# Splits of weights put off by slices, an inverse root in ten steps, casts one per block, coefficients, stabilizer and memory heads placed anew

## The chip, the cores and the metric

The kernel runs on one core of a Trainium2 chip. The metric is the device time of one execution in microseconds; the time of the kernel before is the median of three runs. A NeuronCore has five engines that each take their instructions strictly in the order in which they were written and wait for one another through semaphores: PE (matrix products), DVE and POOL (vectors), ACT (functions and copies) and SP (which here only issues DMA). The order in each engine's queue is therefore part of the kernel, and this change is above all a change of order.

## The reference, cut to what matters

512 tokens of width 1024, in fp32, pass through two transformer blocks.

```python
def first_block(x, ...):
    h = rms_norm(x, attn_norm)
    sb_q, sb_k, sb_v, cq, ckv, k_pe = split(h @ w_in)
    sb  = stick_breaking_attention(sb_q, sb_k, sb_v)          # 8 heads of 64
    mla = chunk_causal_softmax_attention(q, k, v)             # from cq @ w_uq, ckv @ w_ukv, norms, rope
    x = x + concat(rms_norm(sb), rms_norm(mla)) @ w_o
    return x + peer_ffn(rms_norm(x, ffn_norm), ...)           # 16384 experts, 8 heads x top 16

def peer_ffn(h, w_q, sub_keys, u, v):
    sc = einsum(h @ w_q, sub_keys)                            # scores of 2 x 128 keys a head
    idx, g = top 16 of the sums of the two top-16 lists, softmax of their scores
    coef = g * gelu(h . u[idx])
    return sum over k of coef[k] * v[idx[k]]

def second_block(x, c, ...):
    sh1, sc1, g1, sh2, sc2, g2 = split(silu(c) @ w_ada + b_ada)
    hn = rms(x) * (1 + sc1) + sh1
    y  = concat(fox(hn), mlstm(hn), moba(hn))                 # 6 + 4 + 6 heads of 64
    x  = x + g1 * (y @ w_out)
    hn = rms(x) * (1 + sc2) + sh2
    gate, up = split(hn @ w_gate_up)
    return x + g2 * ((silu(gate) * up) @ w_down)
```

`rms_norm` divides by the root of the mean square. The four `mlstm` heads ("memory heads") weigh a product of queries and keys by exp(logd - m), where m, the stabilizer, is a running maximum along the tokens.

## The kernel before

**Products.** An fp32 operand is written as hi + lo, two rounded parts, and `mm3` (L338) makes one product of three matmuls: hi by hi, hi by lo, lo by hi. Weights come through one object, `Stream`: `_load` (L192) has SP issue a DMA of a 128x1024 tile into one of four buffers, `high` (L201) casts it to `whi` on ACT, `_split` (L211) subtracts to make `wlo` on DVE or, for some tiles, on POOL. `get` for tile i splits up to tile i+2 (LOOK = 2), loads up to tile i+5, and then calls `ada_tick`, which advances `ada_gen`: this forms the six modulation vectors of the second block on POOL from tiles `ada_w` that SP loads as well (L638), a unit for each weight tile. `tok_gen` (tokens on partitions) and `feat_gen` (features on partitions) are the generators that take a weight tile and yield after each product of 128 rows of it, a slice; other work is put between slices.

**Norms.** `rsqrt_gen` (L344) makes 1/sqrt on DVE in twelve dependent steps: scale and add, an integer shift, a first guess by a subtraction, three Newton rounds of three steps each. The class `Norm` uses it twice for each of the four row norms: once for three token tiles together (`early`), once for the last tile (`late`).

**The expert layer.** 384 tokens go through all 16384 experts as dense products, with a coefficient that is zero where an expert wasn't chosen; the other 128 tokens gather their rows by indirect DMA. Before the long loop over the 128 first keys stands a stage of 48 blocks (16 for each of three token tiles, `g_hot` and `g_sum`) that builds the matrix of gates G by one-hot products and writes it to memory (`gs` to `gdram`, L1181). Beside the blocks run three steps a block of `decode(1)`, then `decode(2)`, which turn top-k positions into indices on DVE; `spread(2)` (L1044), four ACT casts of indices of 128x1024, is called at block 10. After the stage come `u_next(len(early))`, which makes the first products with u, then loads, then `c_tile(0)` (L1257), which makes the first tile of coefficients: `ch` on ACT, `cl` on DVE. The first product with v needs both.

**The attention of the second block.** 52 items (24 of fox attention, 24 of MoBA, 4 memory heads, put in at the places `ML_AT`) run through `run_pipe`: the parts of an item have lags, counted in items, and between them a `Fill` object takes slices of the generator `behind()`, up to a number of nanoseconds for each item. `behind()` ends with: the stabilizer (`am` on DVE L1547, transposes on PE L1551, a scan on DVE L1553, transposes on PE L1557), the projections `mqk` and `mvo`, the functions silu and sigmoid on ACT, the transposes `y_T(0..4)` (L1536) of the finished parts of y, the first half of the output product. A memory head has a part e (a copy `sel` on DVE L1619, one matmul L1621 that spreads row h of the maximum, four exponentials on ACT), four parts z (a matmul L1634 and a product on DVE L1637 each) and a part v (ten matmuls, L1644).

## Time and profile before

| | |
|---|---|
| runs | 2362.58 us median (2351.52, 2362.58, 2366.8) |
| profiled execution, own time | 2349.11 us |
| its span in the profile | 2347.1 us |
| mean granted clock of PE | 0.979 |
| busy: PE, DVE, ACT, POOL | 2254.4, 1565.1, 964.1, 1008.3 us |

A line of the timeline gives the start, the busy time of the instructions grouped in it, engine, source line, operation, tile written <- tiles read, and in brackets how long the engine stood idle just before and which instruction of which line ended that. A line of the waits adds these up. A clock of 1.00 is 2.4 GHz, 0.50 is 1.2 GHz.

### The profile page before, as it was taken

How to read it: one execution, taken by the hardware profiler on the slowest of the kernel's cores; microseconds unless marked ns; L12 is line 12 of the kernel's file. 1: busy time of each engine (PE TensorE's matmuls, PEld its weight loads, DVE VectorE, ACT ScalarE, POOL GpSimd, SP SyncE). 2: the span in 40 equal slices, each digit the busy share in tenths (PEclk: the TensorE clock that was granted, in tenths of full speed). 3: DMA queues.
4: the chain of work that ended last, by engine and by line, in shares of the span. 5: the costliest groups of instructions: out<-in, count | busy, mean ns of one | idle time of the engine just before them, and what ended most of it. 6: DMA issues, size and time to landing. Idle time of an engine off the chain costs nothing.

```text
span 2347.1 us, 31805 instructions
## 1 busy us (share of the span) xinstructions
PE 2254.4 (96%) x11721; PEld 1935.9 (82%) x11721; DVE 1565.1 (67%) x3005; ACT 964.1 (41%) x1712; POOL 1008.3 (43%) x665
## 2 busy tenths in 40 slices
PE   7999999988989999999999999998999898999999
PEld 6887778988988888888888888888987666888787
DVE  5667659999948888888887888775655245333332
ACT  4567434457843333333333333335543424222211
POOL 5750034620036667676666767624775002600000
PEclk9999999999999999999999999999999879999999
DMA  5430232335798898988989988853442002433231
GB/s 178 140 111 1 81 101 96 102 135 200 283 322 308 308 323 308 317 319 305 347 306 311 321 317 297 308 178 97 138 141 83 29 24 81 153 99 98 86 112 54
DMA packets 175800, 441.09 MB, mean 188 GB/s; under 512 B 17052, under 2 KB 71964, under 8 KB 172572
## 3 DMA queue, kind: packets, MB, share of 16 engines
q1 hardware_dynamic: 136620, 301.87, 38.2%
q0 software_dynamic: 36864, 134.23, 15.7%
q10 hardware_dynamic: 2160, 2.95, 0.5%
q8 instruction: 92, 1.51, 0.3%
q14 instruction: 64, 0.52, 0.1%
HBM read 406.69 MB, written 32.31 MB: 187 GB/s over the span
## 4 chain that ended last, share of the span: by engine, by line
PE 63%; DVE 4%; ACT 3%; issue 2%; DMA 2%; POOL 1%; SPq 0%; ACTq 0%; POOLq 0%; DVEq 0%
PE bank L340 19%; PE bank L342 19%; PE bank L341 19%; PE bank L593 1%; PE bank L582 1%; DVE wlo L211 1%; POOL rows L1286 1%; DVE ohAB L1151 1%; DMA w<-in_peer_v_dram 1%; ACT whi L201 1%; PE bank L574 1%; POOL wlo L211 1%; PE bank L1644 0%; DVE ohA L1158 0%; ACT ohA L1161 0%
## 5 line engine op out<-in xcount | busy, mean ns | idle before, releaser
L340 PE MATMUL bank<-hhi,whi 128*128 128x384 f32 (+1 forms) x1600 | 580.2, 363 | 0.1
L342 PE MATMUL bank<-hhi,wlo 128*128 128x384 f32 (+1 forms) x1600 | 574.3, 359 | 5.7 <-POOL wlo L211 5.7
L341 PE MATMUL bank<-hlo,whi 128*128 128x384 f32 (+1 forms) x1600 | 571.5, 357 | 1.5 <-DVE hlo L466 1.4
L211 POOL TENSOR_TENSOR wlo<-w,whi 128x1024 fp32r<-128x1024 f32 (+2 forms) x128 | 322.0, 2520 | 568.5 <-ACT whi L201 519.4
L201 ACT CAST whi<-w 128x1024 fp32r<-128x1024 f32 (+4 forms) x414 | 421.7, 1024 | 304.1 <-PE bank L342 157.1
L211 DVE TENSOR_TENSOR wlo<-w,whi 128x1024 fp32r<-128x1024 f32 (+3 forms) x286 | 348.4, 1220 | 256.8 <-ACT whi L201 255.9
L342 PEld LDWEIGHTS bank<-hhi,wlo 128*128 128x128 f32 x1600 | 302.8, 189 | 33.7 <-POOL wlo L211 8.7
L340 PEld LDWEIGHTS bank<-hhi,whi 128*128 128x128 f32 x1600 | 302.9, 189 | 31.6 <-issue 4.2
L341 PEld LDWEIGHTS bank<-hlo,whi 128*128 128x128 f32 x1600 | 302.8, 189 | 29.7 <-DVE hlo L466 2.5
L340 PE MATMUL bank<-whi,ch 128*128 128x512 f32 x768 | 303.9, 396 | 5.8 <-ACT ch L1257 4.3
L341 PE MATMUL bank<-wlo,ch 128*128 128x512 f32 x768 | 304.0, 396 | 1.6 <-DVE wlo L211 1.6
L342 PE MATMUL bank<-whi,cl 128*128 128x512 f32 x768 | 304.2, 396 | 0.0
L1264 DVE TENSOR_TENSOR cl<-ge,ch 128x384 fp32r<-128x384 f32 x125 | 145.5, 1164 | 140.2 <-ACT ch L1263 140.2
L1286 POOL DMA_INDIRECT rows<-in_peer_v_dram,eidx x128 | 186.6, 1458 | 119.8 <-DVE acc L1309 87.9
L1286 POOL DMA_INDIRECT rows<-in_peer_u_dram,eidx x128 | 177.4, 1386 | 85.9 <-DVE junk L1304 62.6
L1304 DVE SCALAR_TENSOR_TENSOR junk<-rows,h 128x1024 bf16<-128x1024 f32 x128 | 186.4, 1456 | 0.3
L655 POOL TENSOR_SCALAR ada_w<-ada_w,c_c 128x512 f32<-128x512 f32 x84 | 155.9, 1856 | 70.6 <-DMA ada_w<-in_w_ada_dram 70.5
L1309 DVE SCALAR_TENSOR_TENSOR acc<-rows,coefg,acc 128x1024 f32<-128x1024 f32 x127 | 181.5, 1429 | 0.3
L340 PEld LDWEIGHTS bank<-whi,ch 128*128 128x128 f32 x768 | 144.6, 188 | 37.5 <-ACT ch L1257 4.7
L340 PE MATMUL bank<-whi,hhi 128*128 128x384 f32 (+3 forms) x448 | 174.0, 388 | 0.3 <-ACT whi L201 0.3
L342 PEld LDWEIGHTS bank<-whi,cl 128*128 128x128 f32 x768 | 144.5, 188 | 35.7 <-DVE cl L1264 0.8
L951 ACT ACTIVATE ge<-bank 128x384 f32<-128x384 f32 x113 | 55.7, 493 | 286.1 <-PE bank L342 284.7
(385 smaller groups left out, 3465.9 us busy)
## 6 DMA issues: line engine op xcount, KB each, us to landing
w<-in_uT_dram SPq DMA_DIRECT2D x128, 512.0 KB
w<-in_peer_v_dram SPq DMA_DIRECT2D x128, 512.0 KB
ada_w<-in_w_ada_dram SPq DMA_DIRECT2D x96, 256.0 KB
gdram<-gs SPq DMA_DIRECT2D x24, 1024.0 KB
gblk<-gdram SPq DMA_DIRECT2D x16, 1536.0 KB
w<-in_w_gu_dram SPq DMA_DIRECT2D x44, 512.0 KB
w<-in_w_down_dram SPq DMA_DIRECT2D x22, 512.0 KB
w<-in_w_pq_dram SPq DMA_DIRECT2D x16, 512.0 KB
```

Source lines behind the costliest of these rows:

```text
L201: nc.scalar.copy(hi[:, :n], self.loaded[i][:, :n])
L211: (eng or nc.vector).tensor_tensor(lo[:, :n], t[:, :n], hi[:, :n].bitcast(F32), op=OP.subtract)
L340: nc.tensor.matmul(o, ah, bh, start=start, stop=False)
L341: nc.tensor.matmul(o, ah, bl, start=False, stop=False)
L342: nc.tensor.matmul(o, al, bh, start=False, stop=stop)
L574: nc.tensor.transpose(bt[:, si * P:(si + 1) * P], src()[:, si * P:(si + 1) * P], ident)
L655: nc.gpsimd.tensor_scalar(w, w, col_, None, op0=OP.mult)
L951: nc.scalar.activation(t, b[:, :DTOK], AF.Gelu)
L1264: nc.vector.tensor_sub(cl, t, ch.bitcast(F32))
L1286: nc.gpsimd.indirect_dma_start(out=r, out_offset=None, in_=A["peer_" + kind], in_offset=bass.IndirectOffsetOnAxis(ap=eidx[:, k:k + 1], axi ...
L1304: nc.vector.scalar_tensor_tensor(junk, r, 1.0, h2, op0=OP.mult, op1=OP.mult, accum_out=preg[:, k:k + 1])
L1309: nc.vector.scalar_tensor_tensor(acc, r, coefg[:, k:k + 1], acc, op0=OP.mult, op1=OP.add)
```

## The change

- `Stream.get` has an argument `later`, set by `feat_gen` and by `tok_gen` (but for the last two tiles of an output that is finished token tile by token tile): the cast of tile i+2 is then written behind the first slice, its subtraction and the next load behind the third. The load of tile i+5 so stands behind the `ada_w` load of `ada_tick` in SP's queue.
- `rsqrt_gen`: the shift and the guess become one step; for up to 16 columns the three rounds become a round of five steps with a cubic correction and one of three. Twelve steps become ten, or eleven for wider inputs.
- `spread` becomes a generator: one cast for each of the four blocks from block 10 on, and `decode(2)` makes its first steps behind them.
- `c_tile(0)` stands ahead of `u_next` and of the loads.
- The stabilizer is taken out of its place in `behind()` and put between the slices of `mqk`: `am` ahead of the first slice, the first transposes four slices later, the second ten slices after that.
- Memory heads one item earlier; `sel` becomes a part of its own at lag 0; e, z and v one lag later (1, 3 and 4); `y_T(3)` and `y_T(4)` two MoBA items later.

```diff
-ML_AT = (45, 47, 49, 51)
+ML_AT = (44, 46, 48, 50)
...
+        def step(self):
+            if self.todo:
+                self.todo.pop(0)()
+        def get(self, key, ahead=LOOK, later=False):
...
+            while self.todo:
+                self.step()
             for k in range(i, i + ahead + 1):
-                self._split(k)
-                self._load(k + DEEP - 1)
+                if later and k == i + ahead:
+                    self.todo = [lambda k=k: self.high(k), lambda: None,
+                                 lambda k=k: (self._split(k), self._load(k + DEEP - 1))]
+                else:
+                    self._split(k)
+                    self._load(k + DEEP - 1)
...
-        nc.vector.tensor_scalar(u, v.bitcast(I32), 1, None, op0=OP.logical_shift_right)
-        yield
-        nc.vector.tensor_scalar(u, u, -1.0, 1597463007.0, op0=OP.mult, op1=OP.add)
+        nc.vector.tensor_scalar(u, v.bitcast(I32), -0.5, 1597463007.0, op0=OP.mult, op1=OP.add)
...
-        for k in range(3):
+        cubic = n <= 16
+        for k in range(2 if cubic else 3):
...
+            if cubic and k == 0:
+                nc.vector.tensor_scalar(w, t, 1.5, 2.5, op0=OP.mult, op1=OP.add)
+                yield
+                nc.vector.tensor_mul(t, w, t)
+                yield
...
-            for _ in range(3):
-                next(d, None)
+            if next(sp, sp) is sp:
+                for _ in range(DSTEP):
+                    next(d, None)
...
+        c_tile(0)
         u_next(len(early))
         load_g(0)
         nc.sync.dma_start(h2, x1d[DT])
         bcast_row(acc, A["ffn_norm_row"], D)
-        c_tile(0)
...
-                yield from feat_gen(("mqk", j), hhi, hlo, KC, lambda b: nc.scalar.copy(cv[:, 3:S + 3], b))
+                for ns in feat_gen(("mqk", j), hhi, hlo, KC, lambda b: nc.scalar.copy(cv[:, 3:S + 3], b)):
+                    yield ns
+                    next(st, None)
...
-                yield lambda c=c: step["moba"] >= 8 * (c - 2)
+                yield lambda c=c: step["moba"] >= 8 * (c - 2) + 2
...
-            return [(0, e_part)] + [(2, lambda si=si: z_part(si)) for si in range(NT)] + [(3, v_part)]
+            return ([(0, sel_part), (1, e_part)] + [(3, lambda si=si: z_part(si)) for si in range(NT)] +
+                    [(4, v_part)])
```

Three places show how the order moves. The first is PE's queue at the entry of the memory heads; `ident,y` are the transposes of `y_T`, four each, `mT,sel` is part e, `whi,hhi` and its two neighbours are slices of the other projections, `bv,at_pT`, `ident,at_s` and `kTb,qTb` are MoBA items. Before:

```order
L1536 MATMUL bank<-ident,y 128x128 x8
L582 MATMUL bank<-bv,at_pT 128x64 x4
L574 MATMUL bank<-ident,at_s 128x128 x2
L593 MATMUL bank<-kTb,qTb 128x128
L1536 MATMUL bank<-ident,y 128x128 x12
L644 MATMUL bank<-ones,ada_a 128x1 x4
L340 MATMUL bank<-whi,hhi 128x512
L341 MATMUL bank<-wlo,hhi 128x512
L342 MATMUL bank<-whi,hlo 128x512
L582 MATMUL bank<-bv,at_pT 128x64
L574 MATMUL bank<-ident,at_s 128x128 x3
L1621 MATMUL bank<-mT,sel 128x512
```

Of the change:

```order
L1564 MATMUL bank<-ident,y 128x128 x12
L603 MATMUL bank<-bv,at_pT 128x64 x4
L595 MATMUL bank<-ident,at_s 128x128 x2
L1564 MATMUL bank<-ident,y 128x128 x4
L665 MATMUL bank<-ones,ada_a 128x1 x4
L603 MATMUL bank<-bv,at_pT 128x64
L595 MATMUL bank<-ident,at_s 128x128 x3
L1659 MATMUL bank<-mT,sel 128x512
L614 MATMUL bank<-kTb,qTb 128x128
L603 MATMUL bank<-bv,at_pT 128x64 x2
L595 MATMUL bank<-ident,at_s 128x128 x4
L1564 MATMUL bank<-ident,y 128x128 x4
```

All five groups of transposes stood ahead of the first part e; now the last of them stands behind it, and the slice that stood between them has moved behind the last.

The second place is PE's queue around the stabilizer; `ident,am` and `ident,mT` are its two groups of transposes. Before, two small attention matmuls lie between them:

```order
L593 MATMUL bank<-kTf,qTf 128x512
L1551 MATMUL bank<-ident,am 4x128 x4
L582 MATMUL bank<-fv,at_pT 128x64 x4
L574 MATMUL bank<-ident,at_s 128x128 x2
L593 MATMUL bank<-kTb,qTb 128x128
L1557 MATMUL bank<-ident,mT 128x4 x4
L340 MATMUL bank<-hhi,whi 128x512
```

Of the change, the first group stands among slices of `mqk`, and the second some forty rows further on:

```order
L353 MATMUL bank<-hhi,whi 128x512
L354 MATMUL bank<-hlo,whi 128x512
L355 MATMUL bank<-hhi,wlo 128x512
L1575 MATMUL bank<-ident,am 4x128 x4
L353 MATMUL bank<-hhi,whi 128x512
L354 MATMUL bank<-hlo,whi 128x512
L355 MATMUL bank<-hhi,wlo 128x512
```

Between the two groups there are now ten slices of three matmuls each.

The third is ACT's queue behind the stage of G; `gs` are the last copies of G, `ge` is the gelu of a product with u, `whi` the cast of a weight tile and `ch` the coefficient tile; the numbers are those of buffers. Before:

```order
L1179 COPY gs<-bank 128x128x4 x4
L201 CAST whi<-w_7210 128x1024
L951 ACTIVATE ge<-bank 128x384
L201 CAST whi<-w_7304 128x1024
L951 ACTIVATE ge<-bank 128x384
L1257 ACTIVATE ch<-ge_3318 128x384 x2
L201 CAST whi<-w_7398 128x1024
```

Of the change:

```order
L1204 COPY gs<-bank 128x128x4 x4
L1285 ACTIVATE ch<-ge_3300 128x384
L203 CAST whi<-w_7202 128x1024
L972 ACTIVATE ge<-bank 128x384
L203 CAST whi<-w_7296 128x1024
L972 ACTIVATE ge<-bank 128x384
L1285 ACTIVATE ch<-ge_3300 128x384
```

Two casts and two gelus that stood ahead of the first `ch` now stand behind it.

## Rows read from the trace of the kernel before

**Rows 1.** The page, parts 1 and 5: busy; group, busy, mean ns, idle ahead.

```profile
PE 2254.4 (96%) x11721; PEld 1935.9 (82%) x11721; DVE 1565.1 (67%) x3005; ACT 964.1 (41%) x1712; POOL 1008.3 (43%) x665
...
L340 PE MATMUL bank<-hhi,whi 128*128 128x384 f32 (+1 forms) x1600 | 580.2, 363 | 0.1
```

**Rows 2.** PE's waits: tile and line, what ended the wait: us, times, longest.

```profile
PE bank L434 <- DVE rs_u L349: 22.8, 4, 12.6
PE bank L1536 <- DVE y L604: 7.8, 1, 7.8
...
PE bank L1177 <- ACT ohA L1161: 3.5, 1, 3.5
...
PE bank L340 <- ACT ch L1257: 4.3, 1, 4.3
...
PE bank L1385 <- DVE dg L1391: 2.5, 1, 2.5
...
PE bank L1621 <- DVE sel L1619: 1.9, 3, 0.7
...
PE bank L1557 <- DVE mT L1553: 1.2, 1, 1.2
...
PE bank L1551 <- DVE am L1547: 1.1, 1, 1.1
```

**Rows 3.** Windows: stretch, its length, busy us by engine, clock, DMA share, GB/s.

```profile
538.00:570.00 32.00, 27.97 (x204) 25.70 (x204) 31.12 (x47) 21.85 (x51) 0.00 (x0) 0.89 0.52 182
570.00:660.00 90.00, 89.18 (x822) 85.66 (x821) 81.67 (x106) 71.22 (x167) 0.00 (x0) 1.00 0.77 282
1745.00:1749.00 4.00, 2.08 (x16) 1.65 (x16) 3.24 (x6) 2.60 (x7) 3.80 (x5) 0.99 0.22 71
1749.00:1762.40 13.40, 13.01 (x41) 10.30 (x42) 4.01 (x14) 2.62 (x7) 2.90 (x2) 0.50 0.25 79
1846.40:1861.40 15.00, 15.00 (x44) 10.74 (x44) 4.33 (x13) 6.09 (x14) 1.15 (x4) 0.50 0.11 35
1861.40:1878.60 17.20, 15.13 (x72) 10.03 (x71) 6.79 (x22) 3.96 (x9) 1.14 (x4) 1.00 0.09 31
1878.60:1902.30 23.70, 23.13 (x61) 15.04 (x60) 4.72 (x17) 5.47 (x13) 3.74 (x10) 0.50 0.00 0
1902.30:1922.40 20.10, 17.23 (x97) 12.96 (x96) 9.71 (x35) 2.95 (x5) 1.47 (x2) 0.99 0.09 27
```

**Rows 4.** Timeline of DVE in a norm: first and last of nine chain steps.

```profile
309.25 0.16 DVE L351 TENSOR_SCALAR rs_u<-rs_u 128x3 int32<-128x3 int32 x1
...
311.01 0.16 DVE L360 SCALAR_TENSOR_TENSOR nr_r<-rs_t,nr_r 128x3 f32<-128x3 f32 x1
```

**Rows 5.** Timeline of ACT in the stage of G.

```profile
532.61 3.88 ACT L1044 CAST tir<-topi 128x1024 f16<-128x1024 uint32 x4
```

**Rows 6.** Timeline of ACT at the first coefficient tile.

```profile
672.64 0.94 ACT L1257 ACTIVATE ch<-ge 128x384 fp32r<-128x384 f32 x2 [3.25 <-DMA gdram<-gs]
```

**Rows 7.** Timeline of PE there: the second product with v.

```profile
685.30 0.50 PE L341 MATMUL bank<-wlo,ch 128*128 128x512 f32 x1 [1.60 <-DVE wlo L211]
```

**Rows 8.** Timeline of PE behind the stabilizer: one matmul after the other.

```profile
1750.47 0.63 PE L341 MATMUL bank<-hlo,whi 128*128 128x512 f32 x1
1750.90 0.63 PE L342 MATMUL bank<-hhi,wlo 128*128 128x512 f32 x1
```

**Rows 9.** Timeline of PE in a slice ahead of the memory heads.

```profile
1833.56 0.40 PE L341 MATMUL bank<-wlo,hhi 128*128 128x512 f32 x1
1833.80 0.39 PE L342 MATMUL bank<-whi,hlo 128*128 128x512 f32 x1
```

**Rows 10.** Timeline of DVE at the entry of the memory heads.

```profile
1843.70 1.29 DVE L1538 TENSOR_TENSOR hlo<-bank,hhi 128x512 fp32r<-128x512 f32 x2 [9.48 <-ACT hhi L1537]
```

**Rows 11.** Timeline of DVE ahead of the output of the mixer.

```profile
2195.16 1.23 DVE L211 TENSOR_TENSOR wlo<-w,whi 128x1024 fp32r<-128x1024 f32 x1 [0.25 <-ACT whi L201]
```

**Rows 12.** SP's waits between 1600 and 1850 us.

```profile
SPq L638 <- POOL ada_a L656: 115.8, 33, 18.7
```

More of the change, by code (lines that the diff above doesn't have):

```diff
@@ L68 @@
 PREP_N = 10
+DSTEP = 3
 LOOK = 2
@@ L480, in block @@
                     cp == cps[0] and ci == 0, cp == cps[-1] and ci == per - 1)
+                W.step()
                 yield 3 * N / 2.4
         for cp in cps[:-2] if split else cps:
-            w = W.get((key, cp))
+            w = W.get((key, cp), later=True)
             if not b:
@@ L507, in feat_gen @@
     def feat_gen(key, hi, lo, kc, evac, n=S):
-        wh, wl = W.get(key)
+        wh, wl = W.get(key, later=True)
         b = bank()
@@ L512, in feat_gen @@
             mm3(b[:, :n], (wh[:, w_], wl[:, w_]), (hi[:, c, :n], lo[:, c, :n]), c == 0, c == kc - 1)
+            W.step()
             yield 3 * n / 2.4
@@ L1211, in build @@
                 if tt == 0:
-                    spread(2)
+                    sp = spread_gen(2)
+                    next(sp)
                     ij1, d = decode(2)
@@ L1538, in y_T, with stabilizer @@
             nc.vector.tensor_sub(hlo[:, c, :], b, hhi[:, c, :].bitcast(F32))
+        def stabilizer():
+            nc.vector.tensor_sub(am, gt[:, :, 6:10], cum[:, :, 10:14])
+            for _ in range(4):
+                yield
+            b = bank()
+            for tt in range(NT):
+                nc.tensor.transpose(b[:MLH, tt * P:(tt + 1) * P], am[:, tt, :], ident)
+            nc.vector.tensor_copy(mT, b[:MLH, :])
+            nc.vector.tensor_tensor_scan(out=mT, data0=mT, data1=mT, initial=0.0, op0=OP.max, op1=OP.max)
+            for _ in range(10):
+                yield
+            b = bank()
+            for tt in range(NT):
+                nc.tensor.transpose(b[:, tt * MLH:(tt + 1) * MLH], mT[:, tt * P:(tt + 1) * P], ident[:MLH, :MLH])
+            nc.vector.tensor_add(em, b[:, :16].rearrange("p (t h) -> p t h", t=NT), cum[:, :, 10:14])
+            nc.scalar.activation(em, em, AF.Exp, scale=-1.0)
         def behind():
@@ L1566, in behind @@
             nc.gpsimd.memset(mv1[:, :, :, 64:65], 1.0)
+            st = stabilizer()
             for j in range(4):
```

38 lines of the change are left out of this document (16 added, 22 removed).

## The prediction

> **What bounds the kernel now.** I read the busy times first: PE is busy 2254.4 us of a span of 2347.1 [rows 1], so only 93 us can come back from its waits, and besides them only what it loses at half clock. Then PE's waits one by one, because what the change touches is worth something only where PE stands still: the longest single kinds that it touches are norms, the entry of the memory heads, the first coefficient, and waits of 1 to 3.5 us in between [rows 2]. Then the windows with the granted clock, because behind some of these waits PE runs for 13 to 24 us at 0.50 [rows 3]. The reader is to see that a short wait can be followed by a loss larger than itself. In the long expert loop PE doesn't wait, and the order of all engines there is unchanged, so that part cannot move.
>
> **Norms.** The chain on DVE has nine steps from 309.25 to 311.01, that is (311.01 - 309.25)/9 = 0.195 us a step [rows 4]. A norm has 3 and 1 columns, both below 16, so each of its two chains loses two steps. PE waits for both chains (four waits, 22.8 us in all, begin with one [rows 2]). Per norm 2 x 2 x 0.195 = 0.78, for four norms **-3.1**. Bounds: the late chains lie between other DVE work, so at worst only the early ones count, -1.6; at best a step that waits behind a longer one goes too, -4.
>
> **Stage of G.** Four casts on ACT take 3.88 us in one piece [rows 5], and PE waits 3.5 for the one-hot rows that ACT forms behind them [rows 2]. One cast a block is 3.88/4 = 0.97, and ACT has room: from 538 to 570 it works 21.85 of 32. But DVE works 31.12 of these 32 and PE 27.97, so in this stretch DVE sets the pace, and later, from 570 to 660, PE does (89.18 of 90) [rows 3]. The wait can be saved only so far as DVE follows; its steps of `decode(2)` begin four blocks later, into the stretch where PE leads and hides them. **-3**; bounds 0 (DVE is the bound anyway) and -5 (clock 0.89 there becomes 1).
>
> **First coefficients.** `ch` waits for the last store of `gs` [rows 6], since its tile takes memory from which that store reads; this store isn't sooner, so neither is `ch`. Now ACT, which takes its work strictly in order, holds two casts and two gelus behind it. The first product with v, at about 673 before, behind this `ch`, would come a cast and a gelu or two later, 1 to 2 us. But the second product with v waits for its own `wlo` until 685.30 [rows 7], and that one depends on none of this: the delay goes into its wait of 1.60. **+0.5**; bounds -4.3 (the whole wait of [rows 2], if the store is not what holds it) and +3.
>
> **Stabilizer.** PE waits 1.1 for `am` and 1.2 for the scan [rows 2], 2.3 together. Now four slices and ten slices lie between. Behind these waits it runs 13.4 us at clock 0.50 [rows 3]. A matmul there goes on after 1750.90 - 1750.47 = 0.43 us [rows 8], elsewhere after 1833.80 - 1833.56 = 0.24, or 0.233 over several [rows 9]: a ratio of 1.83. At full clock the 13.01 us of work are 7.1. So 2.3 + 13.4 - 7.1 = **-8.6**; if the clock falls all the same, -2.3.
>
> **Memory heads.** Before, the stretch from the end of PE's work at 1846.4 - 7.8 = 1838.6 to 1922.4 is 83.8 us. The wait of 7.8 [rows 2] stems from ACT: silu, sigmoid and their tables stand ahead of the casts `hhi` of the transposes, and DVE stood still 9.48 us for these before its two `hlo` at 1843.70 [rows 10]. That stays. In the new order PE does more transposes and one MoBA step, and stops where it needs the bank (accumulator tile) of the first transposes, free after the first `hlo`, 1843.70 + 0.65 = 1844.35: a wait of about 5.8, followed by some 1.3 for `sel`, which stands behind three `hlo` (0.65 each). Then comes the work. At full clock the four windows hold 15.00/1.83 + 15.13 + 23.13/1.83 + 17.23 = 53.2 [rows 3]. The first of the two half-clock stretches follows the long wait, which remains, so I leave its loss: 15.00 - 8.2 = 6.8. The second, 23.7 us, came behind three waits of 0.65 to 0.72 for `sel` and for the exponentials, of which rows 2 list `sel` with 1.9. In the new order `sel` is copied an item sooner and slices stand between e, z and v, so I let it go. Of the small waits in these windows, (17.20 - 15.13) + (23.70 - 23.13) + (20.10 - 17.23 - 2.3) = 3.2, I leave a third, 1.0. The 2.3 at the end is a wait for the norm of the heads' result; its chain has 16 columns and loses two steps, 0.4, and begins an item sooner, for which I take off half of the rest: 0.95 stays. Sum 5.8 + 1.3 + 53.2 + 6.8 + 1.0 + 0.95 = 69.0, so **-14.8**. If the second stretch recurs, its loss of 23.1 - 12.6 = 10.5 stays and the term is -4.3.
>
> **Output's modulation.** PE waits 2.5 for `dg` [rows 2], behind a `wlo` of 1.23 [rows 11]; the first two `dg` now stand ahead of it. **-1.4** (with the gap ahead of it); bound 0.
>
> **Splits put off.** The same casts, subtractions and loads, later by one to three slices of 0.7 us (three matmuls [rows 9]). A tile is split two tiles before its use, so PE doesn't see it: **0**. Bounds -2 (PE waits for hi or lo of a slice that no longer stand behind it) and +2 (a subtraction now stands ahead of an attention step). The loads are the third rival.
>
> **Sum.** -3.1 - 3 + 0.5 - 8.6 - 14.8 - 1.4 = -30.4 on the profiled execution of 2349.1 (span 2347.1 and 2.0 around it), so 2318.7 on its own scale. That execution is 13.5 us faster than the median of the runs; against the median I predict 2362.6 - 30.4 = **2332**.
>
> **A rule against it.** The clock part of the sum, 6.3 at the stabilizer (13.4 - 7.1) and 10.5 in the heads, rests on waits of 1.25 us and less that end in half clock; the rows show the falls right behind such waits, at 1749 and at 1878.6, with no longer wait near [rows 2, 3]. The Trainium skill ("TensorE: Matmul & The Clock Gate", section "HAM oscillation") lays a fall to long idle gaps of PE, as where a kernel waits for a transfer between its tiles. By it these two falls would not come from these waits and would not go with them, and the sum would be -30.4 + 16.8 = -13.6. The same page's section on a second failure mode knows falls from many short idles, and there the rows agree, so the page doesn't decide.
>
> **Rivals.**
> 1. *The clock falls anyway*, and not from these waits. PE's work around the falls is narrow: transposes of 4 columns, a matmul with 4 rows, products of 64 rows. If that lowers the clock and not the waits, it falls in the new order too, since these matmuls are all still there. For it: they stand at both places. Against it: from 1861.4 to 1878.6 the same kinds ran at 1.00 [rows 3]. Then both losses remain: -30.4 + 6.3 + 10.5 = -13.6: 2349.
> 2. *Only the heads' second fall recurs*, because z, now one lag later, waits for the exponentials elsewhere. The 1.9 for `sel` [rows 2] would be gone, but ACT still does its sixteen exponentials in the stretch, and their waits were of the same size. -30.4 + 10.5 = -19.9: 2343.
> 3. *Loads come late* (the other side). Some sixty loads of weights stand one `ada_w` load later on SP, and SP waits for POOL's `ada_a` 115.8 us in 33 waits, 3.5 each, at most 18.7 [rows 12]. A load is issued three tiles before its cast; a tile is 8 slices of 0.7, so the lead is some 17 us, less the transfer. A mean wait fits into it, the longest doesn't. If each of sixty loads lost the mean 3.5 with no lead left, it were +210; it decides against the change from 30 + 24 = 54 us on, which is 16 loads with a bare 3.5 each: some 2390. Against it: ahead of its 1600 products of the commonest form PE waited 0.1 us in all [rows 1], so weights are now far from late.
> 4. *The edits do little*: PE's stops move on to the next bank or the next table load, as the entry of the memory heads shows already, and only norms, `dg` and a part of G stay: -3.1 - 1.4 - 3 = -7.5: 2355.
>
> **Chances.** The forecast, all of the sum: 0.45, by itself 2320 to 2342. Rival 1: 0.20; rival 2: 0.18; rival 3: 0.06; rival 4: 0.11. For the range, 2312 takes in the best bounds (-4, -5 and -4.3 instead of -3.1, -3 and +0.5, and the medians' scatter), 2357 the fourth rival. About 1% is what a measurement of this kernel can tell from no change, here 24 us: faster below 2339, slower above 2386. Of the forecast some 0.37 lie below 2339, of rival 2 0.07, of rival 1 0.05: faster 0.49; slower is rival 3, 0.06; the rest is within 1%, 0.45.
>
> **What would show it.** Right: PE's waits for `am` and mT gone and the clock 1.00 in the slices of `mqk`; at the entry of the memory heads one wait near 6 us for a bank, then one half-clock stretch, and none in the middle of the heads; norm waits for `rs_u` shorter by 0.4 each time; no wait of 3.5 for `ohA`; `ch` still behind the last store. Wrong: half clock again behind the stabilizer or in the middle of the heads (rivals 1 and 2); PE's waits for `whi` or `wlo` with a DMA ahead of them (rival 3); the same total of PE's waits under new names (rival 4).

## The result, and the profile after

The changed kernel took 2338.02 us, median of four runs (2319.21 to 2347.63), against 2360.3 for the kernel before (2351.52 to 2366.8): ratio 0.9899, 95% interval 0.9858 to 0.9941. 2332 was forecast, with a range of 2312 to 2357. On two further occasions, six runs each, its medians were 2334.6 and 2329.9, ratios 0.9885 [0.9839, 0.9931] and 0.9871 [0.9828, 0.9915]. Of the 165 runs below, six, all of edited kernels and two of them the changed kernel's (2365.32 and 2362.87), lie more than 1.5% above the fastest of their kernel and are left out of the means as slow; with them the changed kernel's mean would be 2336.9 instead of 2333.0 us and its time at half clock 97.7 instead of 88.7.

The profiled execution has a span of 2336.9 us, 10.2 shorter than the one before, with a mean clock of 0.980. Page, part 1:

```profile
PE 2252.1 (96%) x11721; PEld 1934.5 (83%) x11721; DVE 1562.1 (67%) x2973; ACT 964.8 (41%) x1712; POOL 1000.4 (43%) x665
```

PE's waits (tile and line, what ended the wait: us in all, times, longest). These answer to [rows 2]; the line numbers of the change are 2 to 38 higher.

```profile
PE bank L453 <- DVE rs_u L362: 21.2, 4, 12.1
...
PE bank L595 <- DVE hlo L1566: 6.4, 1, 6.4
...
PE bank L353 <- ACT whi L203: 5.7, 2, 5.4
PE bank L354 <- DVE wlo L213: 5.3, 4, 3.5
...
PE bank L1564 <- DVE y L1645: 1.2, 1, 1.2
...
PE bank L1413 <- DVE dg L1419: 1.0, 1, 1.0
```

The four waits of the norms fell from 22.8 to 21.2, `dg` from 2.5 to 1.0, the heads' last norm from 2.3 to 1.2; `am`, mT, `sel` and the wait of 3.5 for ACT's `ohA` are gone from the list (PE's waits for DVE's `ohA` grew from 7.4 to 9.1 in all). New are 5.4 for `whi` and 3.5 for `wlo` at the first coefficients, where 4.3 for `ch` and 1.6 for `wlo` stood, and the entry of the heads still waits, 6.4 instead of 7.8, now in one go for `hlo`.

Windows of the same execution (stretch, length, busy us by engine, granted clock, DMA share, GB/s), to be read beside [rows 3]: a stretch of the first block that ran at 1.00 before; the slices of `mqk` with the stabilizer; the first half of PE's stand at the entry of the heads (1853.8 to 1860.2); the stretch at 0.50 that begins in this stand; the one behind it.

```profile
211.80:246.00 34.20, 34.20 (x119) 22.57 (x119) 20.29 (x50) 16.66 (x40) 0.00 (x0) 0.50 0.00 1
1744.00:1770.00 26.00, 26.00 (x170) 23.96 (x170) 14.82 (x51) 12.96 (x31) 19.73 (x14) 1.00 0.52 173
1853.80:1857.10 3.30, 0.04 (x1) 0.00 (x0) 0.00 (x0) 3.27 (x6) 0.00 (x0) 0.99 0.00 0
1857.10:1867.30 10.20, 6.52 (x20) 4.42 (x21) 4.55 (x16) 8.62 (x20) 3.95 (x8) 0.50 0.00 0
1867.30:1916.40 49.10, 47.81 (x245) 34.21 (x245) 23.46 (x76) 14.30 (x31) 7.29 (x16) 1.00 0.10 30
```

Behind the stabilizer the clock is 1.00, in the heads 10 us are at 0.50 instead of 44 (before 20.5 from 1841.1 on, in the wait that [rows 3] leaves out, and 23.9 from 1878.6 on), but 34.2 us of the first block's stick-breaking attention ran at 0.50. This stretch hides most of the gain in the profiled execution. So the first thing to find out was which of these stretches belong to the kernel and which to the execution.

### The profile page after: what moved, and what is told of

Same layout as the page of the kernel before. It is cut to its first block, busy times and chain, and to the rows that moved or that the text cites. A ratio compares the mean times of both kernels' runs of the same rounds, so it can differ in the third digit from the quotient of the medians.

```text
span 2336.9 us, 31771 instructions
## 1 busy us (share of the span) xinstructions
PE 2252.1 (96%) x11721; PEld 1934.5 (83%) x11721; DVE 1562.1 (67%) x2973; ACT 964.8 (41%) x1712; POOL 1000.4 (43%) x665
## 4 chain that ended last, share of the span: by engine, by line
PE 79%; DVE 9%; ACT 4%; issue 3%; DMA 3%; POOL 2%; SPq 0%; ACTq 0%; POOLq 0%; DVEq 0%
PE bank L353 23%; PE bank L355 22%; PE bank L354 22%; PE bank L603 2%; PE bank L614 2%; DVE wlo L213 2%; PE bank L595 1%; DMA w<-in_peer_v_dram 1%; DVE ohAB L1176 1%; PE bank L866 1%; DVE ohA L1183 1%; ACT whi L203 1%; POOL rows L1314 1%; POOL wlo L213 1%; PE bank L1051 1%
## 5 line engine op out<-in xcount | busy, mean ns | idle before, releaser
L676 POOL TENSOR_SCALAR ada_w<-ada_w,c_c 128x512 f32<-128x512 f32 x84 | 149.3, 1778 | 75.4 <-DMA ada_w<-in_w_ada_dram 74.9
L354 PEld LDWEIGHTS bank<-wlo,ch 128*128 128x128 f32 x768 | 145.0, 189 | 37.3 <-DVE wlo L213 5.0
```

The costliest lines, as they stand in the source:

```text
L354: nc.tensor.matmul(o, ah, bl, start=False, stop=False)
L676: nc.gpsimd.tensor_scalar(w, w, col_, None, op0=OP.mult)
```

## How the runs are read

Every run lists its span and its mean granted clock c. PE has two levels, so 2(1 - c) times the span is the time it spent at 0.50. Over the 159 runs of all kernels below, with a constant of its own for each kernel, a microsecond at 0.50 goes with 0.447 us of span (standard error 0.012), and the runs scatter by 2.8 us around that line. The difference of two kernels can so be split into a part at half clock and the rest, which is work and waits. In one kernel alone the half clock varies so much (the changed kernel's first four runs have clocks from 0.977 to 0.988, some 108 to 56 us at half clock) that a median over few runs moves by 10 us. "±" is one standard error.

| kernel | runs | mean us | at half clock | rest, against before |
|---|---|---|---|---|
| before | 61 | 2357.4 ± 1.1 | 125.6 ± 2.4 | 0 |
| changed (3 occasions) | 14 | 2333.0 ± 2.6 | 88.7 ± 5.2 | -7.6 ± 0.9 |
| changed, c_tile(0) back | 10 | 2332.4 ± 3.0 | 91.0 ± 6.2 | -9.2 ± 1.0 |
| changed, splits in one piece | 10 | 2335.5 ± 3.6 | 94.8 ± 6.4 | -7.8 ± 1.0 |
| before + stabilizer | 12 | 2352.1 ± 2.4 | 118.4 ± 5.8 | -1.7 ± 0.9 |
| before + heads | 11 | 2343.8 ± 2.7 | 109.1 ± 5.8 | -5.9 ± 0.9 |
| before + both | 12 | 2345.7 ± 2.2 | 116.1 ± 4.5 | -7.2 ± 0.9 |
| pick (e7, e10) | 12 | 2321.6 ± 2.4 | 73.5 ± 5.0 | -12.2 ± 1.1 |
| pick + entry (e8, e11) | 12 | 2324.1 ± 3.1 | 84.5 ± 5.9 | -14.6 ± 1.0 |
| pick + entry + two steps (e9) | 5 | 2320.5 ± 4.3 | 73.3 ± 10.6 | -13.3 ± 1.5 |

The kernel before had 129.3 ± 3.8, 119.3 ± 3.7 and 129.9 ± 5.1 us at half clock on its three occasions (e1 to e4; e5 to e8; e9 to e12), so the half clock of a kernel that ran on one occasion is compared with the runs of before from there.

The second table is worked out from the traces, one of each label: the time between the starts of two products of PE that stand in every kernel, in brackets the us of it at clock 0.50. A: from the first product of the first block to the first score of its attention. B: from there to the first product behind the next norm. G: the stage of G. C: from the end of that stage to the thirteenth slice with v. L: from there to the last slice with v. N: from the first product of the second block to the first of fox attention with values. S: around the stabilizer. H: from the end of the slices before the heads to the last slice of the mixer's output of the first half. F: the gated FFN's first two thirds.

| trace | A | B | G | C | L | N | S | H | F |
|---|---|---|---|---|---|---|---|---|---|
| before | 129.5 | 168.5 (9) | 169.9 (10) | 33.2 (3) | 893.1 | 81.0 | 69.1 (14) | 121.1 (48) | 228.9 |
| changed | 130.9 | 183.1 (43) | 167.9 (12) | 38.6 (10) | 896.5 | 82.0 | 60.8 | 98.2 (10) | 227.0 |
| e1_again | 131.9 (3) | 167.8 (10) | 168.7 (7) | 38.6 (10) | 894.1 | 82.2 | 60.8 | 113.9 (44) | 226.8 |
| e12_again2 | 130.8 | 183.1 (43) | 167.9 (12) | 38.6 (10) | 894.1 | 82.7 (2) | 60.8 | 102.0 (20) | 226.8 |
| e2_ctile_back | 132.3 (3) | 183.1 (43) | 167.9 (9) | 33.5 (7) | 897.2 | 82.4 (1) | 60.8 | 98.6 (10) | 226.8 |
| e3_split_back | 128.3 | 167.7 (9) | 167.9 (9) | 38.6 (10) | 893.3 | 79.4 | 60.8 | 103.3 (20) | 228.3 (1) |
| e4_stab_heads | 129.0 | 183.9 (43) | 169.5 (16) | 33.0 (3) | 894.9 | 80.0 (1) | 60.9 | 118.4 (51) | 228.9 |
| e5_stab_only | 129.0 | 168.3 (10) | 170.2 (14) | 33.6 (3) | 893.9 | 82.8 (3) | 60.8 | 124.8 (55) | 228.9 (1) |
| e6_heads_only | 129.3 | 183.9 (44) | 170.2 (14) | 33.2 (3) | 894.8 | 82.5 (3) | 62.6 | 111.3 (38) | 228.2 |
| e7_pick | 128.8 | 167.1 (7) | 168.4 (10) | 33.1 (7) | 896.2 | 79.9 (1) | 60.8 | 103.3 (20) | 226.8 (1) |
| e10_pick2 | 128.5 | 167.3 (7) | 168.5 (10) | 33.4 (7) | 896.2 | 79.8 (1) | 60.8 | 100.6 (14) | 226.8 (1) |
| e8_entry | 127.7 | 183.1 (43) | 167.9 (9) | 33.5 (7) | 900.0 (3) | 81.0 | 60.8 | 107.4 (34) | 228.6 |
| e11_entry2 | 129.3 | 167.8 (9) | 167.9 (9) | 33.4 (7) | 894.4 | 79.4 | 60.8 | 97.7 (14) | 227.1 |
| e9_steps2 | 128.8 | 167.8 (8) | 168.3 (9) | 33.5 (7) | 894.4 | 79.3 | 60.8 | 97.9 (14) | 227.1 |

## The experiments

### The changed kernel again (e1_again, e12_again2)

No edit.

> The changed kernel once more, nothing edited. In its first trace PE ran 34.1 us at clock 0.50 from about 210 us on, in the stick-breaking attention of the first block, behind a wait of 0.51 us for at_pT; the kernel before has the same wait of 0.51 us at 208.8 us and stayed at 1.00. Theory 'chance of the run': the stretch is there in some executions and not in others, so here it is likely absent from the profile or the runs spread by some 15 us with the mean clock (0.988 without it, about 0.978 with it). Theory 'made by the change' (splits put off shift the work around it): the stretch is there again at 210 us, and no run comes under 2330.

> The changed kernel once more, for a third trace of it. The stretch of 34 us at half clock at 210 us stood in five of ten traces so far, whatever the first block's edits; the fall of the clock in the heads between 10 and 51 us with the new steps. If both are chance, the trace may have either; 37 to 40 us around the first coefficients (30.8 to 33.5 with c_tile back) and 60.8 around the stabilizer must be there again.

Measured: medians 2334.64 (six runs) and 2329.85 (six runs), ratios 0.9885 and 0.9871. The stretch of 34 us is absent from the first of these traces and there in the second (column B: 10, then 43). The first trace of the changed kernel and this one show the same program; windows of e1_again, same columns as above, the first of them the stretch that ran at 0.50 in the first trace, the others in the memory heads:

```profile
211.80:246.00 34.20, 34.15 (x216) 23.17 (x215) 31.14 (x73) 25.50 (x66) 0.00 (x0) 1.00 0.00 1
1837.40:1851.00 13.60, 9.35 (x29) 6.67 (x29) 5.24 (x17) 10.65 (x21) 3.96 (x8) 0.50 0.00 0
1851.00:1854.50 3.50, 3.50 (x14) 2.06 (x13) 1.73 (x4) 0.00 (x0) 0.00 (x0) 0.99 0.00 0
1854.50:1878.30 23.80, 23.80 (x64) 15.94 (x64) 6.48 (x21) 5.35 (x14) 3.99 (x9) 0.50 0.07 23
```

In the first block 34.2 us run at 1.00 here and at 0.50 there, with PE busy 34.15 and 34.20 of them. So that stretch is chance of the execution: over the fourteen traces it stands in six, among them e4 and e6, whose first block is that of the kernel before word for word. It begins 2.0 to 2.5 us behind a wait of half a microsecond; but that wait stands in all fourteen traces, so it doesn't decide. The first trace of the changed kernel, and this one:

```profile
209.36 0.43 PE L603 MATMUL bank<-sbv,at_pT 128*128 128x64 f32 x2 [0.51 <-ACT at_pT L597]
209.64 0.43 PE L603 MATMUL bank<-sbv,at_pT 128*128 128x64 f32 x2 [0.50 <-ACT at_pT L597]
```

The heads are the other way round: this execution ran 23.8 us at 0.50 from 1854.5 on where the first had 1.00, with PE busy every microsecond. PE's timeline ahead of that fall:

```profile
1842.55 2.04 PE L1659 MATMUL bank<-mT,sel 4*128 4x512 f32 x2 [0.57 <-ACT at_pT L597]
...
1851.42 2.42 PE L1672 MATMUL bank<-mqk 64*128 64x512 f32 x8
1853.77 1.45 PE L1659 MATMUL bank<-mT,sel 4*128 4x512 f32 x2
1855.15 1.22 PE L614 MATMUL bank<-kTb,qTb 64*128 64x256 f32 x2
1856.30 0.79 PE L353 MATMUL bank<-whi,hhi 128*128 128x512 f32 x1
```

The last wait of a quarter of a microsecond or more, 0.57, lies 12 us ahead of the fall at 1854.4. Between them PE worked on products of the heads and of attention with no wait above 0.15 us. This fall had no wait right in front of it.

Most falls do have one. Counted over the fourteen traces, from 20 us on to 8 us before the end, each of the 76 waits of PE of 2.7 us or more has a fall of the clock in it or at most 2.1 us behind it; of the 48 waits of 2.0 to 2.7 us that weren't at half clock anyway 33 have one, of the 136 of 1 to 2 us 24. Of all 155 falls 132 stand at such waits. The half clock at long waits is so there in every execution; the stretches of 24 and 34 us, which make executions differ most, have no wait above 0.72 us in the 11 us ahead of them.

### c_tile(0) put back (e2_ctile_back)

```diff
-        c_tile(0)
         u_next(len(early))
         load_g(0)
         nc.sync.dma_start(h2, x1d[DT])
         bcast_row(acc, A["ffn_norm_row"], D)
+        c_tile(0)
```

> The changed kernel with c_tile(0) put back behind u_next and the loads. Theory 'c_tile costs': in the change ACT holds two casts behind the first ch, and PE waits 5.39 us for whi and then 3.47 us for the second wlo, where before it waited 4.35 and 1.60; put back, the two waits return to 4.3 and 1.6 us, and with the 6.8 us at half clock in between back to 3.4, about 4 to 5 us are gained between the stage of G and the loop. Rival, that of the prediction: the second product waits for its own wlo either way, and the place of c_tile is worth 0.5 us.

Measured: stretch C is 38.6 us in the four traces with the early `c_tile(0)` and 33.0 to 33.6 in all ten without: 5.1 us, of which 1.5 to 3 come by the clock (3 to 7 us more at 0.50). In the runs the part outside the half clock falls by 1.7 ± 1.2; the median, 2334.06 (ratio 0.9891 [0.9858, 0.9925]), doesn't show it over the half clock's scatter. The mechanism stands in four views of the changed kernel's first trace. ACT holds the cast behind the coefficients:

```profile
687.09 0.52 ACT L1285 ACTIVATE ch<-ge 128x384 fp32r<-128x384 f32 x1 [8.70 <-DMA gdram<-gs]
687.52 1.03 ACT L203 CAST whi<-w 128x1024 fp32r<-128x1024 f32 x1
```

DVE's split waits for that cast, and its next step for a load (the row of 701.59):

```profile
688.58 1.23 DVE L213 TENSOR_TENSOR wlo<-w,whi 128x1024 fp32r<-128x1024 f32 x1 [0.38 <-ACT whi L203]
701.59 0.17 DVE L1260 SCALAR_TENSOR_TENSOR n<-modc,c_norm_g 128x8 f32<-128x8 f32 x1 [11.78 <-DMA c_norm_g<-in_norm_g_dram]
```

SP issues its next weight load when that split is over and has set a buffer free (688.58 + 1.23 = 689.81, issue at 689.84), 11 us after the load before it, and everything behind it in its queue comes later, `c_norm_g` last:

```profile
678.87 0.37 SPq L194 DMA_DIRECT2D w<-in_uT_dram  x1
689.84 0.33 SPq L194 DMA_DIRECT2D w<-in_peer_v_dram  x1
690.35 0.38 SPq L1274 DMA_DIRECT2D gblk<-gdram  x1
...
695.45 0.43 SPq L313 DMA_DIRECT2D c_norm_g<-in_norm_g_dram  x1
```

So PE waits twice, for the cast and for the second `wlo`, which stands on DVE behind the step that needs `c_norm_g`:

```profile
688.60 0.80 PE L353 MATMUL bank<-whi,ch 128*128 128x512 f32 x1 [5.39 <-ACT whi L203]
...
703.42 0.80 PE L354 MATMUL bank<-wlo,ch 128*128 128x512 f32 x1 [3.47 <-DVE wlo L213]
```

With `c_tile(0)` put back, ACT casts while it waits for the stores; SP's load goes out at 680.64 and `c_norm_g` at 691.50, 3.9 us sooner, though the last store was issued within 0.03 us of the same time (678.45 and 678.42):

```profile
680.64 0.50 SPq L194 DMA_DIRECT2D w<-in_peer_v_dram  x1
686.94 0.38 SPq L1274 DMA_DIRECT2D gblk<-gdram  x1
...
691.50 0.43 SPq L313 DMA_DIRECT2D c_norm_g<-in_norm_g_dram  x1
```

```profile
687.53 0.79 PE L353 MATMUL bank<-whi,ch 128*128 128x512 f32 x1 [4.31 <-ACT ch L1285]
...
699.95 0.50 PE L354 MATMUL bank<-wlo,ch 128*128 128x512 f32 x1 [0.84 <-DVE wlo L213]
```

### Splits in one piece again (e3_split_back)

```diff
-                if later and k == i + ahead:
+                if False and later and k == i + ahead:
```

> The changed kernel with every split and load in one piece again, as before (the argument later has no effect). Prediction: worth 0, with bounds of 2 us each way outside the clock. Rival: the put-off splits change which waits PE has in the first block (0.50 us for wlo at 118 us, 1.28 for m_k at 150) and with them the half clock at 210 us; then the stretch of 34 us is gone from the trace, the time between 65 and 150 us is 2.7 us shorter, and the runs are some 15 us faster.

Measured: the runs as a whole are the same, 2336.55 (ratio 0.991 [0.9872, 0.9948]), the rest -7.8 against -7.6, so on balance the put-off is worth nothing, as forecast. But it is a balance of parts that don't come out at nothing each: A is 130.8 to 132.3 us in the four traces with the put-off and 128.3 here, N 82.0 to 82.7 against 79.4, F 226.8 to 227.0 against 228.3. That would be some 4 us lost in the traces; these runs, with an error of 1.2 on the difference, don't bear out so much, while pick (below), which differs from e2 by the put-off of all tiles but gate and up, has 2.9 ± 1.2 us less than e2. Nor did the put-off make the half clock: 94.8 ± 6.4 us without it, 88.7 ± 5.2 with it. Where A loses is seen at PE's waits: those of 0.25 us or more add up to 3.8 us in the changed kernel's first trace (0.94 and 1.11 for `cqk`, 0.50 for `wlo`, 1.28 for `m_k`) and to 1.8 here (1.01 for `cqk`, 0.79 for `m_k`). The first of them is at the norm of the latent queries. DVE in the changed kernel:

```profile
61.14 1.34 DVE L377 TENSOR_TENSOR rs_t<-rs_t 128x4 f32<-128x4 f32 x2
62.41 1.21 DVE L213 TENSOR_TENSOR wlo<-w,whi 128x1024 fp32r<-128x1024 f32 x1
63.55 0.22 DVE L379 SCALAR_TENSOR_TENSOR lt<-rs_t,rs_u 128x4 f32<-128x4 f32 x2
```

A split of 1.21 us stands between the steps of the inverse root, and PE's transposes, which need the result, wait:

```profile
64.89 0.94 PE L405 MATMUL bank<-ident,cqk 128*128 128x128 f32 x4 [0.94 <-DVE cqk L399]
...
70.63 0.63 PE L405 MATMUL bank<-ident,cqk 128*128 128x128 f32 x4 [1.11 <-DVE cqk L399]
```

In one piece the split stands between the steps of that chain too, two steps sooner:

```profile
59.37 1.22 DVE L213 TENSOR_TENSOR wlo<-w,whi 128x1024 fp32r<-128x1024 f32 x1
```

But from the start of the chain to its first `cqk` it takes 5.09 us here (57.70 to 62.79) and 5.99 there (58.33 to 64.32); over the traces with the ten steps 5.85 to 5.99 in the four with the put-off and 5.03 to 5.57 in the six without it here. So the put-off makes this chain 0.3 to 1.0 us longer; that the split's place among the steps is the reason isn't shown, since it stands in the chain either way. Only the second wait for `cqk` is left here:

```profile
63.36 0.94 PE L405 MATMUL bank<-ident,cqk 128*128 128x128 f32 x4
...
69.01 0.63 PE L405 MATMUL bank<-ident,cqk 128*128 128x128 f32 x4 [1.01 <-DVE cqk L399]
```

### Stabilizer and heads alone (e4_stab_heads, e5_stab_only, e6_heads_only)

The kernel before with the edits of the change to the stabilizer, to the heads, or to both (their diffs stand in the section on the change), nothing else.

> The kernel before with two parts of the change alone: the stabilizer between the slices of mqk, and the memory heads one item earlier with sel at lag 0, e, z, v at 1, 3, 4, and y_T(3), y_T(4) two items later. If these two parts carry the gain, the second block from 1680 to 1925 us becomes some 30 us shorter, as in the changed kernel (it went from 24 us behind to 6 us ahead of the kernel before), and the whole kernel is 23 to 30 us faster than before (ratio 0.987 to 0.990). If the other parts were needed for it, less than 15 us.

> The kernel before with the stabilizer alone put between the slices of mqk. In all five traces that have this edit the stretch around it takes 60.8 us and has no half clock, against 69.1 us and 13.7 at 0.50 in the one trace without it. Theory 'the waits are the cause and the fall is regular': here too 60.8 us and none at half clock, the runs 8 us faster than before (ratio 0.996 to 0.997), and the mean clock of the runs gives some 14 us less at half clock. Rival 'chance': the fall at 1749 was one of those that come in some executions and not in others; then the runs gain only the two waits, 2.3 us.

> The kernel before with the steps of the memory heads alone. With the time at half clock taken off (0.44 us for each us at 0.50), the heads' stretch took 100.1 us before and 93.7 to 95.8 with the edit in five traces, so 5 us of waits are gone. At half clock it had 47.8 us before and 10.2, 44.4, 10.2, 20.5 and 51.2 with the edit. Theory 'waits in the heads make the clock fall' (the prediction's): the runs lose some 24 us at half clock on average, 15 us faster than before in all. Rival 'the fall comes without waits': in one trace of the changed kernel it came at 1854 us with no wait of 0.25 us near; then the time at half clock over the runs stays that of the kernel before and only 5 us are gained (ratio 0.998). The stretch around the stabilizer, unedited, shows a second time whether the fall at 1749 is regular: 13.7 us at half clock or none.

Measured: both 2348.64 (ratio 0.9946 [0.9919, 0.9972]), the stabilizer alone 2352.21 (0.9998 [0.9968, 1.0027]), the heads alone 2345.94 (0.9948 [0.9915, 0.9981]). In waits the two add up, -1.7 and -5.9 against -7.2 together. But they don't carry the gain: both together took 13.4 ± 2.7 us off the mean of their occasion (2359.1 to 2345.7), where 23 to 30 were expected if they did and less than 15 if not. For the stabilizer the rival is right: the mean went from 2354.4 ± 1.7 to 2352.1 ± 2.4 on its occasion, the half clock from 119.3 ± 3.7 to 118.4 ± 5.8, so it is worth its two waits. The second trace without the edit, that of e6, has both waits in PE's timeline and no fall behind them:

```profile
1761.70 0.60 PE L1551 MATMUL bank<-ident,am 128*4 128x128 f32 x4 [1.07 <-DVE am L1547]
...
1764.40 0.38 PE L1557 MATMUL bank<-ident,mT 4*128 4x4 f32 x4 [0.63 <-DVE mT L1553]
```

```profile
1764.00:1778.00 14.00, 13.60 (x69) 10.22 (x70) 7.44 (x21) 5.71 (x14) 5.76 (x4) 1.00 0.31 95
```

So the 13.7 us at half clock in the trace of the kernel before don't come each time. They began at 1748.9, in the second wait, which took 1.25 us there and 0.63 here. No fall stood in stretch S in any of the twelve traces with the edit, so it may be rarer there now; the runs of e5, with 1 ± 7 us less at half clock than before on their occasion, leave that open. The heads lose 6 us of waits. In the traces their half clock is 48 and 55 us with the old steps, 51 and 38 in e4 and e6, whose heads have the new ones, and 10 to 44 in the other ten. In the runs it fell by 13 ± 6 us in e4 and 10 ± 7 in e6, so the expectation of e6 is not decided: 10.6 ± 3.2 us in all lie between its 15 and its 5.

### What was worth keeping (e7_pick, e10_pick2)

c_tile(0) back as above, and

```diff
-                if later and k == i + ahead:
+                if later and key[0] in ("gate", "up") and k == i + ahead:
```

> The changed kernel with c_tile(0) put back and the put-off of splits left on for the gate and up tiles alone (where it brings dg ahead of a split). From the segments: c_tile back is worth 5.1 us less (stretch around it 33.5 instead of 38.6), splits in one piece 2.5 us less in the first block and 2.2 in the second, while the last stretch keeps its 226.8 to 227.0 us (228.0 with all splits back). Theory 'the parts add up': some 9 to 10 us faster than the changed kernel outside the half clock, a median of about 2327 and a ratio to before of 0.986. Rival: parts overlap and it is no faster than with c_tile alone back.

> The kernel e7_pick once more, beside the changed kernel on one chip. With the time at half clock taken off it stood at 2286.3 us against 2291.2 for the changed kernel (ten runs of two calls). If the parts put back are worth 5 us, that difference is seen again, and its median lies below the changed kernel's whatever the clock does; if its 2317.0 was luck of the clock (76 us at half clock against 100), the medians come within 5 us of each other.

Measured: 2317.01 (0.9872 [0.9829, 0.9916]) and 2319.95 (0.9837 [0.9803, 0.987]), the second beside the changed kernel's 0.9871 on the same chip. The parts are all there in the traces: A 128.5 to 128.8, N 79.8 to 79.9, C 33.1 to 33.4, F 226.8. In the runs they come to 4.6 ± 1.1 us less outside the half clock than the changed kernel, about half of the 9 to 10 that were expected; column L, 896.2 in both traces, takes some of it back against the 894.1 of two traces of the changed kernel, and the rest isn't explained. The half clock is lower too, 73.5 ± 5.0 against 88.7 ± 5.2, of which C accounts for 3 us. Taken together 2321.6 ± 2.4 against 2333.0 ± 2.6.

### The entry of the heads (e8_entry, e11_entry2)

As pick, and

```diff
             def ev_mvo(tt, b):
                 nc.scalar.copy(mv1[:, tt, :, 0:64], ...)
-                nc.scalar.copy(og[:, tt, :], b[:, 256:512])
-            yield from tok_gen("mvo", hhi, hlo, KC, 512, ev_mvo)
-            for j in range(4):
-                nc.scalar.activation(mqk[:, j, :], mqk[:, j, :], AF.Silu)
+                mvb.append(b)
+            for n_, ns in enumerate(tok_gen("mvo", hhi, hlo, KC, 512, ev_mvo)):
+                if n_ == 16:
+                    for j in range(4):
+                        nc.scalar.activation(mqk[:, j, :], mqk[:, j, :], AF.Silu)
+                yield ns
             for tt in range(NT):
-                nc.scalar.activation(og[:, tt, :], og[:, tt, :], AF.Sigmoid)
+                nc.scalar.activation(og[:, tt, :], mvb[tt][:, 256:512], AF.Sigmoid)
```

> As the kernel e7_pick, and the entry of the memory heads relieved on ACT: the four silu are written behind the sixteenth slice of mvo, and the sigmoid reads the accumulator itself, so that four copies, one table load and 2.2 us of silu no longer stand between the projection and the casts hhi. Theory 'ACT's queue holds the entry': the wait of 6.38 us for hlo shrinks by about 4.6 to 1.8 us, and if the fall of the clock behind it (10 to 14 us at 0.50) comes from that wait, it goes too, another 4 to 6 us. Rival 'the clock falls there anyway': only the 4.6 us, with some 10 us at half clock still behind the entry.

> The kernel e8_entry once more. Its median was 15 us above that of e7_pick, though its wait at the entry of the memory heads is 1.35 us instead of 6.38; it had 100 us at half clock against 76, 34 of them in the first block, which the edit doesn't touch. Theory 'chance of the clock': on this chip it is 2 to 5 us faster than e7_pick with the half clock taken off, and the half clock over the runs is alike. Rival: the edit brings more half clock in the heads (34 us there against 20.5), and it is slower again.

Measured: 2332.19 (0.9897 [0.9855, 0.9939]) and 2318.88 (0.9819 [0.9784, 0.9855]). The wait of 6.38 is down to 1.35 (PE's timeline of e8_entry; 0.92 in e11):

```profile
1844.84 0.44 PE L595 MATMUL bank<-ident,at_s 128*128 128x128 f32 x2 [1.35 <-ACT mvo L1623]
...
1848.34 1.19 PE L1663 MATMUL bank<-mT,sel 4*128 4x512 f32 x1 [0.41 <-DVE sel L1658]
```

The clock fell all the same, 1.4 us behind it, and a second time in the middle of the heads, where PE was busy for all of 23.9 us (windows):

```profile
1846.20:1856.40 10.20, 9.79 (x33) 7.11 (x32) 6.11 (x18) 7.68 (x15) 2.62 (x7) 0.50 0.00 0
1856.40:1870.00 13.60, 13.60 (x68) 9.13 (x66) 5.07 (x18) 2.53 (x7) 1.14 (x4) 1.00 0.12 40
1870.00:1893.90 23.90, 23.90 (x62) 15.54 (x61) 7.04 (x21) 6.81 (x15) 3.00 (x9) 0.50 0.07 22
```

Outside the half clock this is 2.4 ± 1.2 us better than pick, half of the 4.6 of the first expectation and at the low end of the 2 to 5 of the second; the half clock is 84.5 ± 5.9 against 73.5 ± 5.0 over the runs, on the occasion of e11 alone 68.7 ± 4.6 against 71.2 ± 7.0, and the second trace has 14 us in the heads as pick has. So queue and wait are right, the hope for the clock isn't borne out, and whether it beats pick can't be told: 2324.1 ± 3.1 against 2321.6 ± 2.4.

### Two steps of decode beside a block (e9_steps2)

As the last, with `DSTEP = 2`.

> As the kernel e8_entry, with two steps of decode beside a block instead of three. In the stage of G the change wins 3.2 us in its first part (48.4 to 45.2) and gives 1.2 back in its second (121.5 to 122.6), where PE waits 1.89 and 1.41 us for ohA behind DVE's steps of decode(2), which begin later than before. Theory 'DVE is overfilled for some blocks': with two steps a block these waits shrink and the second part falls to 121.5 or below. Rival: the steps only last longer and the drain at block 10 stalls PE instead; the second part stays at 122.6 or more.

Measured: 2321.34 (0.9839 [0.9799, 0.9878]); G is 168.3 against 167.9, so nothing is won. In the changed kernel PE waits in the second part of the stage behind DVE's steps:

```profile
573.40 0.23 PE L1201 MATMUL bank<-ohA,ohAB 128*128 128x128 f16 x1 [1.89 <-DVE ohA L1183]
...
582.86 0.23 PE L1201 MATMUL bank<-ohA,ohAB 128*128 128x128 f16 x1 [1.41 <-DVE ohA L1183]
```

With two steps a block those shrink (to 1.05 and 0.72), but `decode(1)` isn't done by block 10, and the drain there holds PE for `ij`, 2.19 and 4.06 us, where it waited for nothing before:

```profile
524.40 0.30 PE L1157 MATMUL bank<-ident,ij 128*128 128x128 f32 x1 [2.19 <-DVE ij L1121]
528.77 0.45 PE L1157 MATMUL bank<-ident,ij 128*128 128x128 f32 x1 [4.06 <-DVE ij L1121]
```

Divided where the expectation divides it, the first part of the stage went from 45.2 to 49.3 us and the second from 122.6 to 119.0. So the theory is right for the second part, which fell below 121.5, and the rival for the drain; the two cancel. Three steps up to block 10 and two behind it weren't run; by these two parts (45.2 + 119.0 against 167.9) they would be worth some 3.7 us, an estimate.

## Why the prediction was right or wrong, step by step

The whole came out: -24.4 us in the means (2357.4 to 2333.0) against -30.4, and -7.6 outside the half clock plus (125.6 - 88.7) x 0.447 = -16.5 by the clock, where the sum had -13.6 and -16.8. That the clock's part came out is luck: the two stretches that it was priced from are not what the runs gained. The other parts:

- **Norms, -3.1.** Right. The eight waits of the four norms in the first traces add up to 31.2 before (12.56, 3.24, 3.14, 2.05, 3.14, 1.87, 3.94, 1.30) and 28.2 after (12.08, 2.84, 2.76, 1.67, 2.75, 1.61, 3.59, 0.92): -3.0, spread over early and late chains alike.
- **Stage of G, -3.** Mechanism right: the wait of 3.5 for ACT's rows is gone. Mis-sized: -2.0 (169.9 to 167.9; -3.2 in the first part, +1.2 in the second). The steps of `decode(2)`, said to be hidden where PE leads, make PE wait 1.89 and 1.41 us at 573 and 583.
- **First coefficients, +0.5.** Wrong; stretch C went from 33.2 to 38.6 us, 5.4 and beyond the upper bound of 3, some 3 of it by the clock (7 us more at 0.50). The failing step is "that one depends on none of this". The second `wlo` depends on it by a ring that the working didn't follow: ACT's cast, DVE's split, the weight buffer that it frees, SP's next load, and behind that in SP's queue the load of `c_norm_g`, for which a DVE step ahead of the `wlo` waits. That `ch` itself waits for the last store was right: 687.09, behind `gdram`.
- **Stabilizer, -8.6.** The waits, 2.3, were right within their error (-1.7 ± 0.9 in the runs; 62.6 to 60.8 in the traces without a fall). The 6.3 at half clock are the failing step: a stretch that one execution showed was taken for a property of the kernel, and e5's runs have no less half clock than before.
- **Memory heads, -14.8.** The entry was read rightly, a wait near 6 us for the bank (6.38) and then a small one (0.57 instead of 1.3), with half clock in it and behind it, as at every wait of that length. Waits outside the clock -5.9 ± 0.9 in e6, where the sum had -14.8 + 10.5 = -4.3. The 10.5 by the clock has the wrong reason: falls come in the middle of the heads with the new steps too, and without waits. How many there are differs by execution; the first trace of the changed kernel, which had none there, would have seemed to prove the step right.
- **Output's modulation, -1.4.** Right: the wait for `dg` went from 2.5 to 1.0, and is 2.5 again when the splits go back (F 228.3 against 226.8 to 227.0).
- **Splits put off, 0.** Right within the error in the runs of e3, though pick is 2.9 ± 1.2 us below e2; wrong in the reason given, since PE does see them, at the norm of the latents among others. The upper bound of 2, a subtraction ahead of an attention step, came nearest to that. The loads, the third rival, cost nothing that showed: PE's list of waits has no weight load.
- **The long loop.** The working had it at nothing, since its order is unchanged. Column L is 893.1 before and 894.1 to 896.5 in the three traces of the changed kernel, 1 to 3 us more at full clock that nothing here explains.

Of the rivals, the first, that the clock falls anyway and not from these waits, is right for the heads, where it fell in e1 without them; at the stabilizer it fell in one of two traces with the old order and in none of twelve with the new. That narrow matmuls make it fall, as this rival supposed, wasn't tested. Its time of 2349 did not come, because the half clock went down all the same, by 37 ± 6 us on average. By the rule that the prediction weighed (the Trainium skill, "TensorE: Matmul & The Clock Gate", section "HAM oscillation") the two falls would not go with the short waits; where PE did wait long, the traces agree with it (76 of 76), and e1 agrees that the heads' fall needs no short wait; but the long gap of PE that the rule names instead wasn't there either, since PE was busy 23.80 of 23.80 us from that fall on and had no wait above 0.15 us for 11 us ahead of it.

**What stays open.** Where the 37 us of half clock went. The stabilizer and the heads alone took 13 ± 6 away, the remaining parts the rest, though in stretch C they add 7. The norms and the stage of G were never run by themselves. The four traces without them (before, e4, e5, e6) all have a stretch of 24 or 34 us at 0.50 in the middle of the heads, of the ten with them two, e1 and e8, have it; nothing here shows why. One trace of a kernel doesn't give the mean of a stretch. Nor was it tried what in the heads' and in the attention's work makes the clock fall where no long wait stands.

## What to carry to other kernels

Price a wait from the trace, but a stretch at half clock that no long wait explains only from several executions: regress the runs' spans on their mean clock and compare what is left over, which told 2 us apart where medians moved by 10. When an instruction is put ahead of others on an engine, follow what it holds up round the whole ring, to the buffers that the held work frees and to the loads that stand behind these in the DMA queue. Where work that is put off lands should be looked up in the trace: the chain that the busiest engine waited for became 0.3 to 1.0 us longer by it.

## What the runs showed of the hardware

TensorE's clock fell from 2.4 to 1.2 GHz at each of 76 waits of TensorE of 2.7 us or more, in the wait or at most 2.1 us behind it. It also fell without a long wait: for 34 us in the stick-breaking attention in six of fourteen traces, each time 2.0 to 2.5 us behind a wait of half a microsecond that the other eight traces have too; and in the memory heads for 24 us in five traces (before, e1, e4, e6, e8), in four of them with no wait above 0.15 us in the 11 us ahead, and for 34 us in a sixth (e5), right behind a wait of 0.72. In the long loop of dense products, 893 to 900 us, it stood at 1.00 in thirteen of fourteen traces. The kernel before spent 98 to 161 us at half clock in the 61 runs beside the experiments, and a us of it costs 0.447 us.
